# A float32 matmul with bias and tanh: another order of row tiles and column banks in the opening

## The chip, the cores and the metric

One core of one Trainium2 chip. The metric is the device time of one execution in microseconds (us); the profile's span is some 1.7 us shorter than it. "Product" below means one matmul instruction of 128x128 weights and 512 columns; the kernel needs 8192 of them (the last 32 are cut in two halves each).

## The reference

```python
def setup_inputs():
    m, k, n = 4096, 4096, 4096
    return {"a": randn(m, k), "b": randn(k, n), "bias": randn(n)}   # all float32; cut

def reference(a, b, bias):
    return np.tanh(np.matmul(a, b) + bias)
```

## The kernel before

A is loaded by GpSimd with a cast to fp16, transposed by VectorE in 32x32 blocks and held as `at` (k on the partitions). B's columns go in four groups of 1024, each two PSUM banks wide. Once a group of B is in SBUF, a row tile takes 64 products. The *opening* is the first 8 row tiles of the first column group: 512 products, made while B and A are still arriving, so it cuts k into pieces and keeps partial sums aside in SBUF (`spill`).

```python
    P, Q, QP, NB = 128, 4, 32, 512
    KT, MT, NCW, J = 32, 32, 1024, 2
    G = 4; KS = 8; AN = 3; BL = 4; KM = 16; WARM = 9
    ...
    def put_aside(ps, m, j):                      # first partial sum
        nc.scalar.copy(aside(m, j), ps)

    def add_aside(ps, m, j):                      # a further one
        nc.vector.tensor_tensor(out=aside(m, j), in0=ps, in1=aside(m, j), op=add)

    def end(ps, m, j):                            # last one: add, tanh, store
        finish(ps, aside(m, j), m, j * NB, o_sb=aside(m, j))

    def across(ps, ms, t0, nt, first):            # 4 rows x 2 banks, k tile by k tile
        for t in range(t0, t0 + nt):
            for m in ms:
                for j in range(J):
                    mm(ps[m][j], ats[m], b_cur, t, j, t == first, False)

    def group1(t0, t1, done, before):             # rows 4 to 7, one after the other
        for m in range(G, 2 * G):
            for j in range(J):
                ps = psum.tile([P, NB], fp32, name="ps")
                for t in range(t0, t1):
                    mm(ps, ats[m], b_cur, t, j, t == t0, t == t1 - 1)
                before(m, j)
                done(ps, m, j)

    for i in range(WARM):                         # products on zeros, to warm the array
        nc.tensor.matmul(warm, zeros[:, :P], zeros, start=i == 0, stop=i == WARM - 1)

    load_b_low(nc.sync, raw_b, 0, 0, 1)           # k tile 0 of B as float32
    nc.scalar.copy(b_cur[0][:, 0, :], raw_b[:, 0, :])
    for m in range(G):
        load_nat(m, 1)                            # A, k 0 to 4, by rows
    ...                                           # B k 1 to 2, A k 4 to 8, B k 3 to 6, ...
    turn_nat(0, 1, nc.vector.tensor_copy)         # transposed on TensorE
    turn_nat(1, 1, nc.scalar.copy)
    row(0, 0, 1)
    ...                                           # cut
    group1(KM, KT, end, before3)                  # last block: rows 4 to 7, k 16 to 32
```

`want(...)` puts a load in a list that GpSimd issues in order; a load of A waits for one of AN = 3 buffers. `turn(...)` is the VectorE transpose of a loaded piece.

## Time and profile before

| | before |
|---|---|
| median, 4 runs | 1785.2 us (1784.98 to 1785.65) |
| span of the profile | 1783.5 us |
| first product | 6.79 us |
| 65th product starts | 25.30 us |
| 513th product starts (opening over) | 121.99 us |
| from there to the last column | 1654.2 us, 0.2154 us each |

The prediction below shows the lines. The starts of the nth product are counted from the matmul records of the trace, of which none is missing; 512 products at 0.2158 us are 110.5 us. How to read them: TensorE is the chain from 23.73 us to the end, so only the opening's first 25 us can be shortened, and only if nothing later starts to wait. That condition is what this case is about.

### The profile page before, as it was taken

The page shows a single profiled execution, that of the slowest core. Times are in us where ns is not written, and L with a number is a line of the kernel's source. Part 1 is how long each engine was busy: PE and PEld are TensorE (multiplying, and loading weights), DVE is VectorE, ACT ScalarE, POOL GpSimd, SP SyncE. Part 2 cuts the span into 40 slices and gives each one's busy share as a digit, 9 for nine tenths or more (in the row PEclk, how much of TensorE's full clock was granted, in tenths as well). Part 3 has the DMA queues.
Part 4 walks back from the last instruction along what each step waited for, and adds up shares of the span by engine and source line. Part 5 has one row for each costly group of instructions (what it writes and reads, how often), then busy time and mean ns, then how long its engine had stood idle before and what let it go on. Part 6 is the DMA issues. An engine that isn't in the chain of part 4 may idle for free.

```text
span 1783.5 us, 20856 instructions
## 1 busy us (share of the span) xinstructions
PE 1774.8 (100%) x8257; PEld 807.3 (45%) x8257; DVE 768.3 (43%) x686; ACT 173.8 (10%) x279; POOL 865.1 (49%) x1611
## 2 busy tenths in 40 slices
PE   8999999999999999999999999999999999999999
PEld 3444444444444444444444444444444444444444
DVE  2864444344434443444434443444334443444342
ACT  2021000000000000000000000000000000000001
POOL 6455666544465445444455555444544454444510
PEclk9999999999999999999999999999999999999999
DMA  9999999876999967767699997766777667766731
GB/s 189 204 178 174 173 167 161 137 134 108 160 172 165 152 109 117 116 111 128 111 169 170 159 151 116 119 117 107 129 115 123 107 111 118 119 114 109 116 77 42
DMA packets 280321, 238.68 MB, mean 134 GB/s; under 512 B 157856, under 2 KB 230560, under 8 KB 280224
## 3 DMA queue, kind: packets, MB, share of 16 engines
q0 software_dynamic: 242784, 169.71, 69.5%
q1 hardware_dynamic: 37152, 67.52, 10.6%
q8 instruction: 64, 1.05, 0.2%
q14 instruction: 33, 0.27, 0.0%
q10 hardware_dynamic: 288, 0.13, 0.0%
HBM read 337.64 MB, written 67.11 MB: 227 GB/s over the span
## 4 chain that ended last, share of the span: by engine, by line
PE 98%; DMA 1%; issue 0%; POOL 0%; ACT 0%; DVE 0%; POOLq 0%; DVEq 0%
PE ps L415 93%; PE ps L138 6%; DMA b<-in_b_dram 1%; POOL nat L238 0%; ACT o_sb L152 0%; POOL b L69 0%; DVE o_sb L149 0%; PE tp L251 0%; POOL ident L257 0%; POOLq L257 0%; DVEq L149 0%; POOLq L438 0%
## 5 line engine op out<-in xcount | busy, mean ns | idle before, releaser
L415 PE MATMUL ps<-b,at 128*128 128x512 f16 x7712 | 1657.8, 378 | 0.0
L90 POOL DMA_DIRECT2D an<-in_a_dram x1488 | 800.2, 545 | 802.0 <-DVE at L100 570.0
L415 PEld LDWEIGHTS <-at 128*128 128x128 f16 x7712 | 754.6, 98 | 903.3
L100 DVE STREAM_TRANSPOSE at<-an 128x3072 f16<-128x3072 f16 (+2 forms) x376 | 563.1, 1548 | 50.5 <-DMA an<-in_a_dram 50.5
L149 DVE TENSOR_TENSOR o_sb<-ps,bias_bc 128x512 f32<-128x512 f32 (+1 forms) x243 | 165.8, 683 | 919.0 <-PE ps L415 711.4
L152 ACT ACTIVATE o_sb<-o_sb 128x512 f32<-128x512 f32 (+1 forms) x243 | 151.4, 624 | 1502.6 <-DVE o_sb L149 1496.6
L73 POOL DMA_DIRECT2D b<-in_b_dram x96 | 51.8, 544 | 17.8 <-DMA an<-in_a_dram 9.1
L138 PE MATMUL ps<-b,at 128*128 128x512 f16 x256 | 56.9, 379 | 3.0 <-DMA b<-in_b_dram 2.6
L138 PE MATMUL ps<-b,atx 128*128 128x512 f16 x256 | 55.7, 379 | 0.0
L138 PEld LDWEIGHTS <-at 128*128 128x128 f16 x256 | 24.7, 98 | 33.2 <-issue 3.5
L138 PEld LDWEIGHTS <-atx 128*128 128x128 f16 x256 | 25.1, 98 | 30.2
L100 DVE STREAM_TRANSPOSE atx<-an 128x512 f16<-128x512 f16 (+2 forms) x14 | 17.7, 1300 | 10.2 <-DMA an<-in_a_dram 10.2
L69 POOL DMA_DIRECT2D b<-in_b_dram x13 | 8.3, 641 | 22.3 <-PE ps L415 19.8
L152 ACT ACTIVATE spill<-spill 128x512 f32<-128x512 f32 x16 | 10.1, 630 | 76.8 <-DVE spill L149 76.8
L149 DVE TENSOR_TENSOR spill<-ps,spill 128x512 f32<-128x512 f32 x16 | 11.0, 687 | 15.1 <-PE ps L138 15.1
L175 DVE TENSOR_TENSOR spill<-ps,spill 128x512 f32<-128x512 f32 x16 | 10.2, 677 | 3.2 <-PE ps L138 3.2
L172 ACT COPY spill<-ps 128x512 f32<-128x512 f32 x16 | 8.8, 593 | 22.0 <-PE ps L138 21.9
L180 DVE TENSOR_TENSOR spill<-spill,bias_bc 128x512 f32<-128x512 f32 x16 | 9.7, 678 | 0.0
L225 PE MATMUL ps<-zeros 128*128 128x512 f16 x9 | 4.0, 631 | 1.3 <-DVE zeros L221 1.3
L252 DVE COPY atx<-tp 128x1024 f16<-128x1024 f16 x1 | 0.7, 692 | 7.2 <-PE tp L251 7.2
L252 DVE COPY at<-tp 128x512 f16<-128x512 f16 x2 | 0.8, 425 | 5.9 <-PE tp L251 5.9
L238 POOL DMA_DIRECT2D nat<-in_a_dram x5 | 2.8, 574 | 1.1 <-POOLq L438 0.8
(14 smaller groups left out, 12.4 us busy)
## 6 DMA issues: line engine op xcount, KB each, us to landing
an<-in_a_dram POOLq DMA_DIRECT2D x480, 192.0 KB, 4.9
out_dram<-o_sb SPq DMA_DIRECT2D x239, 256.0 KB, 2.4
an<-in_a_dram POOLq DMA_DIRECT2D x960, 32.0 KB, 2.6
b<-in_b_dram POOLq DMA_DIRECT2D x103, 256.0 KB, 8.3
b<-in_b_dram POOLq DMA_DIRECT2D x6, 1024.0 KB, 13.5
out_dram<-spill SPq DMA_DIRECT2D x16, 256.0 KB, 2.3
an<-in_a_dram POOLq DMA_DIRECT2D x28, 128.0 KB, 6.4
an<-in_a_dram POOLq DMA_DIRECT2D x12, 256.0 KB, 7.6
```

What stands on the lines that cost most here:

```text
L69: queue.dma_start(out=dst, in_=src[:, ds(t0 % BL, nt), :])
L73: nc.gpsimd.dma_start(out=bt[t0 // TB][ds(q * QP, QP), ds(t0 % TB, nt), :], in_=src.rearrange("(t p) n -> p t n", p=QP),)
L90: nc.gpsimd.dma_start(out=an[ds(q * QP, QP), :, ds((t - t0) * QP, n * QP)], in_=src.rearrange("(mb p) k -> p mb k", p=QP),)
L100: nc.vector.transpose(at[:, ds(t, n), :].rearrange("P t (mb p) -> P mb t p", p=QP), an[:, ds(mb0, Q), ds((t - t0) * QP, n * QP)].rearrange ...
L138: nc.tensor.matmul(ps, at[:, t, :], bt[t // TB][:, t % TB, ts(j, NB)], start=start, stop=stop)
L149: nc.vector.tensor_tensor(out=o_sb[:, piece], in0=ps[:, piece], in1=addend[:, piece], op=mybir.AluOpType.add)
L152: nc.scalar.activation(o_sb[:, piece], o_sb[:, piece], mybir.ActivationFunctionType.Tanh)
L172: nc.scalar.copy(aside(m, j), ps)
L175: nc.vector.tensor_tensor(out=aside(m, j), in0=ps, in1=aside(m, j), op=mybir.AluOpType.add)
L180: nc.vector.tensor_tensor(out=aside(m, j), in0=aside(m, j), in1=bias_bc[:, ts(j, NB)], op=mybir.AluOpType.add)
L225: nc.tensor.matmul(warm, zeros[:, :P], zeros, start=i == 0, stop=i == WARM - 1)
L415: nc.tensor.matmul(ps, at[:, t, :], b_cur[t // TB][:, t % TB, ds(c0, w)], start=t == 0, stop=t == KT - 1,)
```

## The change

Its intent: let TensorE begin with less data. Eight row tiles by one bank of columns use the same eight PSUM banks as four rows by two, but a step from bank 0 to bank 1 then needs only 0.5 MB of new data for 32 products. The first 0.5 MB of B (k 0 to 4 of bank 0) comes through SyncE as float32 and is cast by ScalarE, row tiles of A are worked on as they land. Sizes in MB are 2^20 bytes as written to SBUF, fp16 unless said otherwise.

```diff
-    G = 4
+    R = 8
+    H = R // 2
...
-    raw_b = spill[3]...[:, ds(0, 1), :]
-    load_b_low(nc.sync, raw_b, 0, 0, 1)
-    nc.scalar.copy(b_cur[0][:, 0, :], raw_b[:, 0, :])
+    raw = bpool.tile([P, BL, NB], fp32, name="raw", tag="b_3")
+    for t in range(0, BL, 2):
+        load_b_low(nc.sync, raw[:, ds(t, 2), :], 0, t, 2, NB)
+    for t in range(BL):
+        nc.scalar.copy(b_cur[0][:, t, :NB], raw[:, t, :])
...
+    want_a("a0", R - NN, NN * P, (R - NN) * Q, 0, BL)      # rows 6 and 7
+    want(lambda: load_b_bank_low(1, 0, 2))
+    want(lambda: load_b_bank_low(1, 2, 2))
+    want(lambda: load_b_bank_low(1, BL, BL))
+    want_half(0, BL, BL)                                   # A of rows 0 to 3
+    want_half(1, BL, BL)                                   # A of rows 4 to 7
+    want(lambda: load_b_bank_low(0, BL, BL))
+    want_half(0, 8, 4)
+    want(lambda: load_b_bank(0, 8, 4))
+    want_half(1, 8, 4)
+    want_half(0, 12, 4)
+    want(lambda: load_b_bank(0, 12, 4))
+    want_half(1, 12, 4)
+    want(lambda: load_b_bank(1, 8, 4))
+    want(lambda: load_b_bank(1, 12, 4))
+    want(lambda: load_bias(bias_bc, 0, nc.gpsimd))
+    for t in (KM, KM + 8):
+        want(lambda t=t: load_b_bank(1, t, 4))
+        want_half(0, t, 8)
+        want(lambda t=t: load_b_bank(1, t + 4, 4))
+        want_half(1, t, 8)
+    for t in range(KM, KT, 4):
+        want(lambda t=t: load_b_bank(0, t, 4))
...
+    for m in rows:                                         # bank 1, k 24 to 32
+        row(ps, m, 1, KM + 8, KT, done=end)
...
-    group1(KM, KT, end, before3)
+    for i, m in enumerate([*range(H, R), *range(H)]):      # last block: bank 0, k 16 to 32
+        row(ps, m, 0, KM, KT, start=True, done=end)
+        if i in (2, 5):
+            new_at(i // 3)
```

The visits are, as (bank, k): (0, 0 to 4), (1, 0 to 8), (0, 4 to 16), (1, 8 to 32), (0, 16 to 32).

## The prediction

> **What bounds the kernel now.** I read the page first, then the chain that ended last in order of time, then the timeline of TensorE over the first 30 us, then two windows. From the page:
>
> ```profile
> span 1783.5 us, 20856 instructions
> PE 1774.8 (100%) x8257; PEld 807.3 (45%) x8257; DVE 768.3 (43%) x686; ACT 173.8 (10%) x279; POOL 865.1 (49%) x1611
> PE 98%; DMA 1%; issue 0%; POOL 0%; ACT 0%; DVE 0%; POOLq 0%; DVEq 0%
> ```
>
> TensorE is 98% of the chain. Nothing outside TensorE can be worth more than the other 2%. The chain in order of time says where those are:
>
> ```profile
> 4.47 6.72 DMA b<-in_b_dram
> ...
> 12.86 8.71 DMA b<-in_b_dram
> 21.57 0.04 issue
> 21.61 1.67 PE ps L138 x7
> 23.29 0.45 PE tp L251 x8
> 23.73 98.42 PE ps L138 x456
> 122.15 1654.20 PE ps L415 x7680
> ```
>
> From 23.73 us on TensorE runs without a wait: 456 matmuls in 98.42 us and 7680 in 1654.20 us, 0.2158 and 0.2154 us each. Before 23.73 us the chain goes through loads of B. The timeline of TensorE there (start, length, engine, line, count, idle time before with its releaser):
>
> ```profile
> 5.08 0.63 PE L251 MATMUL tp<-ident,nat 128*128 128x128 f16 x4
> 6.54 0.41 PE L251 MATMUL tp<-ident,nat 128*128 128x128 f16 x4 [0.83 <-DMA nat<-in_a_dram]
> 6.79 0.59 PE L138 MATMUL ps<-b,at 128*128 128x512 f16 x2
> ...
> 9.14 4.35 PE L138 MATMUL ps<-b,at 128*128 128x512 f16 x18 [0.25 <-ACT at L252]
> 15.31 5.56 PE L138 MATMUL ps<-b,at 128*128 128x512 f16 x25 [1.83 <-DMA b<-in_b_dram]
> 21.61 1.67 PE L138 MATMUL ps<-b,at 128*128 128x512 f16 x7 [0.74 <-DMA b<-in_b_dram]
> 23.12 0.61 PE L251 MATMUL tp<-ident,nat 128*128 128x128 f16 x8
> 23.57 1.89 PE L138 MATMUL ps<-b,at 128*128 128x512 f16 x8
> 25.30 4.91 PE L138 MATMUL ps<-b,atx 128*128 128x512 f16 x22
> ```
>
> The first real matmul starts at 6.79 us and 64 are done at 25.30 us. At 0.2158 us, 64 take 13.8 us, so 4.7 us of these 18.5 us are lost: 2.57 us in the two named waits for B, the rest in 16 transposes (0.4 to 0.6 us a group) and matmuls whose operand was just copied. So the budget has three parts: 6.79 us before the first product, 4.7 us lost to 25.30 us, and some 3.7 us after the last matmul (1783.5 minus 1779.83, where TensorE's last piece ends). The third is untouched. The ideal gain of any opening is a few us of 1785: 2% would be 35.7 us.
>
> The rate of the loads sets the opening:
>
> ```profile
> 6.79:23.73 16.94, 13.97 (x76) 6.33 (x75) 2.91 (x5) 2.88 (x6) 10.13 (x18) 1.00 1.35 188
> 23.73:122.15 98.42, 98.42 (x458) 44.64 (x456) 67.17 (x79) 16.54 (x28) 51.01 (x94) 1.00 1.14 197
> ```
>
> The last figures are the DMA share and GB/s as written (fp16, so twice that is read): the engines are full throughout, and TensorE still keeps up after 25 us, if each byte comes in the right order. Summing the trace's packets of the GpSimd queue by their ends: 0.25 MB by 5.4 us, 0.5 by 7.0, 0.75 by 8.6, 1.0 by 10.1, 1.5 by 13.1, 2.0 by 15.6, 2.5 by 18.1, 3.0 by 20.6, 3.5 by 23.5, 14.25 by 78.3. An instruction sees its data 0.4 to 1 us after the last packet.
>
> **What the Trainium skill says.** (1) "TensorE: Matmul & The Clock Gate", Back-to-back issue gap: the isolated gap of warm matmuls of 512 columns is about 216 ns. The trace agrees (0.2154 to 0.2158 us), so the change's 8192 matmuls cost the same. The same section gives 131 ns for sustained streams; this trace shows nothing near it. (2) "DMA: Bandwidth & Descriptors", SWDGE vs HWDGE vs iDMA: a cast inside a DMA is only possible from GpSimd. That is why B through SyncE arrives as float32 and needs ScalarE copies. (3) The same page, Issuing engines are not separate DMA queues: queues share the same 16 engines. The trace agrees: in the us where both queues were busy (3.5 to 4.5 us) SyncE's wrote 148 KB and GpSimd's 124 KB, against some 340 and 170 KB alone.
>
> **The change part by part.**
>
> *Removed.* The order of 4 rows by 2 banks. For its first 32 products it needed 512 rows of B by 1024 columns, 1 MB as fp16, and 0.5 MB of A; for 64, 3 MB; these are what the two waits are for.
>
> *Added.* Eight rows by one bank: the first 32 products need 1 MB of A and 0.5 MB of B, the second 32 only 0.5 MB more of B, the third 1 MB of A and 0.5 MB of B, the fourth 0.5 MB of B. So 64 products need 2.0 MB instead of 3, and 128 need 4 in both. B's first 0.5 MB is 1 MB of float32 by SyncE, 0.5 MB more than before in that form.
>
> *Loads.* SyncE's first half should be there at 4.4 us as its 0.5 MB was before; the second half costs 0.5/0.34 = 1.5 us of engine time, shared with GpSimd's loads, so it comes at some 7 us and the GpSimd curve above shifts by up to 1.5 us. With 0.9 us to landing: A's first rows at 5.4, 7.2, 8.2, 9.3, 10.1 and 10.9 us; rows 6 and 7 (0.25 MB) 12.4; B's second bank, first halves, 13.9 and 15.4, then 18; A of k 4 to 8 for rows 0 to 3 20.5, rows 4 to 7 23.0; B bank 0 of these 25.9 us.
>
> *ScalarE.* Four casts of 128x512 instead of one of 128x1024 that took 1.05 us: about 0.55 each, done by about 5.5 and 8.7 us. Evictions take 0.59 us alone (8 in a row took 4.23), under a row's 0.86 us. *VectorE:* six copies of 0.42 us, two small transposes of about 0.65 us. Both lie beside TensorE.
>
> *TensorE.* Row 1's transposes start at 7.2 us. Row 0 k 0 to 1 from 7.5, row 1 from 8.1 (its copy), row 2's transposes to 9.0, k 2 to 3 of rows 0 and 1 to 9.9; then rows 2, 3, 4 at 0.86 + 0.3 to 0.4 us for the next row's transposes, to 13.5; rows 5, 6, 7 at 0.86, to 16.1 us. Each row's data are there by then. Bank 1 for all rows: 32 times 0.216 = 6.9 us, to 23.0 us, its last B having come at 15.4. The third block has its A at 20.5 and 23.0 plus 0.65 to 2.6 us of VectorE, needed at 23.0 and 26.5.
>
> Sum: 64 products at 23.0 us instead of 25.3, gain 2.3 us, and no transpose of TensorE after it in either kernel. The 8128 products left and the end are the same. 1785.3 minus 2.3 = 1783.0 us.
>
> **The rivals.**
>
> *A. A wait later in the opening.* A of k 8 to 16 now comes in runs of 4 k tiles (256 B written; packets of that size went at 177 KB/us, 512 B at 194, 2 KB at 208) and B in 1 KB (195 KB/us). I put some 57 us between 3.5 and 14.25 MB, slightly slower than before's 54.8. Estimated margins: k 16 to 24, rows 4 to 7: loaded 65, needed 71; k 24 to 32, rows 4 to 7: 82 with its transpose, needed 85; bank 0 of k 16 to 32: 90, needed piece by piece from 91.7. In that last stretch eight outputs of 256 KB go out (before, 8 of them went in 90 to 97 us), which may cost B 3 us. For: the margin there is about zero. Against: the kernel before had no wait at all after 25 us at nearly the same load. This would give back 1 to 4 us: 1784 to 1787.
>
> *B. SyncE's float32 starves A.* If SyncE's queue takes the larger share, row 1 lands after 7.5 us and everything slips by 1 us; if GpSimd's does, k 2 to 3 comes at 9 to 10 us. Either takes 0.5 to 1.5 us: 1783.5 to 1784.5.
>
> *C. PSUM or the buffers.* Eight rows use all eight banks, and a stage's row m waits for the eviction of its row m of the stage before. A stage goes row by row, so seven rows lie between (6 us against 0.7). Against it also: VectorE's in-order transposes precede the evictions, but their loads are due before. Spill tiles take slots of tiles read for the last time in the first block. I expect no wait. If one of these were wrong at every stage change: +5 us.
>
> *D. A better start.* If rows come as early as before (6.5 us), the gain is 3.5 to 4: 1781.5.
>
> **Range and chances.** Centre 1783.0. D gives 1781, A and C at their likely sizes up to 1786.5; 8 in 10: 1780.8 to 1786.2. Faster by 2% is impossible by the budget (15 us in all): 0.005. Slower by 2% needs 36 us of new waits in a 120 us opening whose loads are the same: 0.015. Within 2%: 0.98.
>
> **What would show it.** In the changed profile: first product at about 7.5 us; casts of 128x512 near 4.5 and 7 us; the 65th product at 23.0 plus or minus 1 us; no wait of TensorE for B over 0.5 us before it; from there one unbroken piece in the chain of waits to the last column. The prediction is wrong if TensorE waits for A or B between 23 and 120 us (rival A), if the first block ends after 17 us (B), if TensorE waits for VectorE or ScalarE at a stage change (C), or if the time per matmul is not 0.2154 to 0.2158 us.

## The result, and the profile after

| | before | after |
|---|---|---|
| median, 4 runs each | 1785.2 us | 1786.67 us |
| lowest to highest | 1784.98 to 1785.65 | 1784.24 to 1788.93 |
| ratio, after over before | | 1.0008 (95%: 0.999 to 1.0025) |

A ratio is the mean time of one kernel's runs over that of the other's runs of the same rounds, so not quite the ratio of the medians quoted. The median lies 0.5 us above the predicted range, and the spread of the kernel after is 4.7 us where that of before is 0.7. The profile is of its slowest run (1788.93 us). Its page:

```profile
span 1787.2 us, 20871 instructions
PE 1777.3 (99%) x8257; PEld 807.9 (45%) x8257; DVE 764.8 (43%) x693; ACT 174.2 (10%) x280; POOL 883.2 (49%) x1629
PE 94%; DMA 4%; POOL 1%; issue 1%; ACT 0%; DVE 0%; DVEq 0%; POOLq 0%
```

TensorE is 94% of the chain where it was 98%: the chain now runs through loads for much longer. The chain in order of time shows how long (start, length, what):

```profile
46.93 7.59 DMA bias_bc<-in_bias_dram
...
77.95 7.67 DMA an<-in_a_dram
85.62 1.56 issue
87.18 4.28 POOL b L74 x8
91.47 7.40 DMA b<-in_b_dram
98.87 0.14 issue
99.00 26.88 PE ps L139 x116
125.89 1654.20 PE ps L391 x7680
```

Before, TensorE's unbroken piece began at 23.73 us; now it begins at 99.00 us, released by a load of B. From there the rest is the same to a hundredth: 1654.20 us. So the whole difference lies in the opening. TensorE's timeline of the kernel after:

```profile
7.08 0.62 PE L236 MATMUL tp<-ident,nats 128*128 128x128 f16 x4 [1.80 <-DMA nats<-in_a_dram]
8.08 0.61 PE L236 MATMUL tp<-ident,nats 128*128 128x128 f16 x4 [0.38 <-DMA nats<-in_a_dram]
8.49 1.91 PE L139 MATMUL ps<-b,atx 128*128 128x512 f16 x4
...
17.23 1.89 PE L139 MATMUL ps<-b,atx 128*128 128x512 f16 x8
...
24.19 3.63 PE L139 MATMUL ps<-b,atx 128*128 128x512 f16 x16
...
80.46 7.08 PE L139 MATMUL ps<-b,atx 128*128 128x512 f16 x32 [0.84 <-DVE atx L101]
87.38 9.66 PE L139 MATMUL ps<-b,at 128*128 128x512 f16 x44
99.00 13.07 PE L139 MATMUL ps<-b,at 128*128 128x512 f16 x52 [1.97 <-DMA b<-in_b_dram]
```

The two waits for B before 25 us are gone, and the 65th product starts at 24.19 us instead of 25.30. But two new waits stand at 80.46 us (A of k 24 to 32 for rows 0 to 3, turned late by VectorE) and 99.00 us (the last piece of B's first bank). Why the first of them was late, VectorE's timeline shows:

```profile
69.84 4.62 DVE L101 STREAM_TRANSPOSE at<-an 128x1024 f16<-128x1024 f16 x4 [3.33 <-DMA an<-in_a_dram]
74.39 4.86 DVE L183 TENSOR_TENSOR spill<-spill,bias_bc 128x512 f32<-128x512 f32 x8
79.17 4.62 DVE L101 STREAM_TRANSPOSE atx<-an 128x1024 f16<-128x1024 f16 x4
```

The last load of that A was in at 77.67 us (the chain above: 70.00 + 7.67), but VectorE had the bias additions of bank 1 ahead of it in its program and turned it only from 79.17 us. Those additions themselves stood behind A of rows 4 to 7, which landed just before 69.84 us. So this wait comes from late loads and from the place of the additions together; 1.5 us of it is the additions.

And 52 products from 99.00 us end at 111.91, where the next piece starts: 12.9 us for what takes 11.2 at 0.2158. The windows around it say why; the last three figures are the granted clock, the DMA share and GB/s:

```profile
90.00:95.00 5.00, 5.00 (x25) 2.29 (x24) 5.00 (x9) 4.02 (x7) 3.58 (x7) 1.00 1.09 140
95.00:100.00 5.00, 3.04 (x13) 1.14 (x12) 4.99 (x9) 0.82 (x2) 2.80 (x6) 0.91 1.17 289
100.00:105.00 5.00, 5.00 (x18) 1.96 (x17) 0.69 (x1) 0.63 (x1) 3.10 (x6) 0.74 1.24 289
```

The granted clock is 0.91 and 0.74 there. The trace's clock record has it at one half from 99.15 us for 3.41 us: the wait of 2 us was answered by a halved clock just as the data arrived. The Trainium skill, "TensorE: Matmul & The Clock Gate", Part 1, describes such a gate, half rate after an idle window of some 3.4 us; the length of the period, 3.41 us, agrees, but here 2 us of idle time were enough (see e5).

The ledger of this profile, each term as the distance between products less 0.2158 us: start of the 65th product 1.1 us earlier; wait at 80 us 1.0 us; wait at 99 us 2.1 us; half clock 1.7 us. Sum +3.7 us, and the spans differ by 1787.2 - 1783.5 = 3.7 us.

**When the loads are in.** Summing the packets of GpSimd's queue by their ends gives, for the same number of MB:

| MB | 0.125 | 0.5 | 1.5 | 2.5 | 3.5 | 7 | 11 | 14.25 | 16 |
|---|---|---|---|---|---|---|---|---|---|
| before, us | 4.6 | 7.0 | 13.1 | 18.1 | 23.5 | 41.8 | 61.6 | 78.3 | 88.2 |
| after, us | 6.2 | 8.5 | 14.3 | 20.8 | 27.3 | 48.2 | 68.2 | 85.4 | 97.6 |

The queue after is 1.5 us late from the start, 4 us at 3.5 MB and 7 us at 14.25 MB. The table is not yet a cause: before, the last 2 MB hold only A for rows 4 to 7, due later.

### The profile page after: what moved, and what is told of

Its sections match the earlier page's. It is cut to its first block, busy times and chain, and to the rows that moved or that the text cites. A ratio compares the mean times of both kernels' runs of the same rounds, so it can differ in the third digit from the quotient of the medians.

```text
span 1787.2 us, 20871 instructions
## 1 busy us (share of the span) xinstructions
PE 1777.3 (99%) x8257; PEld 807.9 (45%) x8257; DVE 764.8 (43%) x693; ACT 174.2 (10%) x280; POOL 883.2 (49%) x1629
## 4 chain that ended last, share of the span: by engine, by line
PE 94%; DMA 4%; POOL 1%; issue 1%; ACT 0%; DVE 0%; DVEq 0%; POOLq 0%
PE ps L391 93%; DMA an<-in_a_dram 2%; PE ps L139 2%; DMA b<-in_b_dram 1%; POOL b L74 1%; POOL an L91 0%; DMA bias_bc<-in_bias_dram 0%; DMA nats<-in_a_dram 0%; POOL b L70 0%; ACT o_sb L153 0%; POOL nats L231 0%; DVE o_sb L150 0%; DVEq L150 0%; POOLq L414 0%
## 5 line engine op out<-in xcount | busy, mean ns | idle before, releaser
L101 DVE STREAM_TRANSPOSE at<-an 128x3072 f16<-128x3072 f16 (+2 forms) x382 | 564.4, 1528 | 16.2 <-DMA an<-in_a_dram 16.2
L74 POOL DMA_DIRECT2D b<-in_b_dram x120 | 65.3, 550 | 11.5 <-issue 5.3
L101 DVE STREAM_TRANSPOSE atx<-an 128x512 f16<-128x512 f16 (+1 forms) x20 | 16.7, 892 | 19.9 <-DMA an<-in_a_dram 19.9
L70 POOL DMA_DIRECT2D b<-in_b_dram x10 | 7.4, 743 | 20.5 <-PE ps L391 19.6
L150 DVE TENSOR_TENSOR spill<-ps,spill 128x512 f32<-128x512 f32 x16 | 10.3, 677 | 11.4 <-PE ps L139 11.4
L178 DVE TENSOR_TENSOR spill<-ps,spill 128x512 f32<-128x512 f32 x8 | 4.8, 673 | 0.0
```

The lines of the kernel that those rows point to most:

```text
L70: queue.dma_start(out=dst, in_=src[:, ds(t0 % BL, nt), :])
L74: nc.gpsimd.dma_start(out=bt[t0 // TB][ds(q * QP, QP), ds(t0 % TB, nt), ds(c0, w)], in_=src.rearrange("(t p) n -> p t n", p=QP),)
L101: nc.vector.transpose(at[:, ds(t, n), :].rearrange("P t (mb p) -> P mb t p", p=QP), an[:, ds(mb0, Q), ds((t - t0) * QP, n * QP)].rearrange ...
L150: nc.vector.tensor_tensor(out=o_sb[:, piece], in0=ps[:, piece], in1=addend[:, piece], op=mybir.AluOpType.add)
```

## The experiments

**The theories.** *L*: the new opening's loads are slower, for their small pieces, and TensorE runs into them. *Q*: a form of it, that GpSimd holds back small loads while a large one is under way. *S*, the rival: only the start counts and the rest is noise. Two more were formed: *H*, that part of the first block runs at half clock, and *D*, that the load order's deadlines matter more than its rate.

All edits are to the kernel after unless said otherwise. All sixteen gave correct results, each with five runs beside nine runs of the kernel before on the same chip. The columns: median and spread; the median of before; then of the profiled run the starts of the 33rd, 65th and 513th product. The runs were made in four calls on three chips (e1 to e4; e5 to e8; e9 to e12; e13 to e16), so medians are best compared within a call, or with the kernel before of the same call.

| run | median (lowest to highest) | before | 33rd | 65th | 513th |
|---|---|---|---|---|---|
| e1_again | 1786.44 (1785.9 to 1789.45) | 1785.39 | 17.46 | 24.37 | 126.25 |
| e2_a8 | 1784.88 (1784.67 to 1786.57) | 1785.39 | 18.84 | 25.75 | 122.44 |
| e3_split | 1786.58 (1784.91 to 1789.01) | 1785.39 | 17.27 | 24.18 | 121.73 |
| e4_sync_half | 1783.98 (1782.23 to 1787.41) | 1785.39 | 17.93 | 24.83 | 124.14 |
| e5_warm | 1787.7 (1785.49 to 1788.63) | 1785.3 | 15.95 | 23.85 | 125.45 |
| e6_before_narrow | 1785.5 (1784.96 to 1785.97) | 1785.3 | 16.69 | 24.95 | 121.64 |
| e7_a8_warm | 1784.89 (1784.51 to 1787.72) | 1785.3 | 16.24 | 23.77 | 122.85 |
| e8_a8_sync | 1786.69 (1784.92 to 1789.73) | 1785.3 | 17.21 | 24.12 | 122.91 |
| e9_chunk | 1784.88 (1783.92 to 1785.53) | 1785.52 | 17.64 | 24.55 | 122.35 |
| e10_chunk_warm | 1783.26 (1782.9 to 1784.66) | 1785.52 | 15.84 | 22.74 | 120.08 |
| e11_chunk_a8_bias | 1784.12 (1783.48 to 1785.54) | 1785.52 | 16.83 | 23.74 | 120.43 |
| e12_all | 1783.95 (1783.44 to 1787.98) | 1785.52 | 15.36 | 22.27 | 120.19 |
| e16_again_2 | 1785.44 (1784.64 to 1789.26) | 1785.62 | 17.57 | 24.48 | 122.78 |
| e15_chunk_warm_2 | 1783.85 (1783.69 to 1785.17) | 1785.62 | 15.89 | 22.80 | 120.52 |
| e13_late_loads_warm | 1783.96 (1783.05 to 1787.0) | 1785.62 | 15.56 | 22.47 | 120.13 |
| e14_all_warm | 1783.53 (1782.97 to 1785.23) | 1785.62 | 16.76 | 24.01 | 121.96 |

No interval of a ratio excludes 1: the smallest ratios are 0.9989, of e10 (0.9976 to 1.0001) and e14 (0.9975 to 1.0002). So the argument rests on the profiles' waits and on sets of runs that do not overlap, not on the ratios.

### e1_again: no edit

> The changed kernel again, unedited, as the yardstick of this call. Theory L (loads): the new opening finishes its first 64 products about 1 us earlier than before, but its loads run later than before from 15 us on (14.25 MB of the GpSimd queue by 85.4 us against 78.3), so TensorE waits near 80 and 96 us, and a wait of about 2 us there is followed by 3.4 us at half clock. It expects 1784 to 1789 us, with the spread of the four runs known. Theory S (start): only the first block matters, and the four runs known are noise: 1784 to 1785 with a spread under 1 us.

Measured: 1786.44 us with a spread of 3.6 us, nine runs of before beside it within 1.2. In its profile TensorE waited 3.4 us for the last B at 99.5 us and was at half clock twice, from 8.1 and 100.3 us. The pattern of the first profile repeats, and the spread belongs to the kernel. S in its simple form (1784 to 1785, spread under 1) is out.

### e2_a8: A of k 8 to 16 in larger pieces

```diff
-    want_half(0, 8, 4)
+    want_half(0, 8, 8)
     want(lambda: load_b_bank(0, 8, 4))
-    want_half(1, 8, 4)
-    want_half(0, 12, 4)
+    want_half(1, 8, 8)
     want(lambda: load_b_bank(0, 12, 4))
-    want_half(1, 12, 4)
```

(and the transposes to match)

> A of k 8 to 16 in pieces of 8 k tiles (packets of 512 B) instead of 4 (256 B), nothing else. Theory L with packet size as the cause: 2 MB at about 194 instead of 175 KB per us, so all later loads come some 1.1 us earlier, the waits near 80 and 96 us shrink by that much, 1 to 3 us faster than the unedited kernel (about 1784). Theory Q (issue order: at most eight GpSimd loads under way, so small loads behind a large one leave the queue short): fewer and larger pieces help as well, up to 2 us. Theory S: no difference.

Measured: 1784.88 us, 1.6 under e1. 7 MB are in at 45.0 us, against 46.8 (e1) and 48.2 (after); 14.25 MB at 83.1 against 84.2 and 85.4. TensorE has no wait after the first block. The chain that ended last, in order of time:

```profile
15.55 107.05 PE ps L139 x496
122.60 1654.20 PE ps L387 x7680
```

One unbroken piece from the first block to the end, though the first block itself was slow (the 33rd product at 18.84 us; see e5). Larger pieces do bring the data sooner, by 1.1 to 1.9 us against e1 (16 MB at 93.8 us against 97.2), and in this profile the waits are gone. TensorE also came 1.4 us later to them (65th product at 25.75 us), which helps. L and Q both predict it.

### e3_split: the two 512 KB loads of B halved

```diff
-    want(lambda: load_b_bank_low(1, BL, BL))
+    want(lambda: load_b_bank_low(1, BL, 2))
+    want(lambda: load_b_bank_low(1, BL + 2, 2))
...
-    want(lambda: load_b_bank_low(0, BL, BL))
+    want(lambda: load_b_bank_low(0, BL, 2))
+    want(lambda: load_b_bank_low(0, BL + 2, 2))
```

> The two loads of 512 KB of B for k 4 to 8 are each cut into two of 256 KB; packets, bytes and order stay. Theory Q: GpSimd's wait of 4.4 us at 20.7 us shrinks to under 2, 3.5 MB of the queue are in by 26 us instead of 27.3, and the kernel gets 1 to 2 us faster. Theory L with packet size as the cause: the wait of GpSimd changes, but the rate stays at some 160 to 175 KB per us between 15 and 28 us, and the time stays within 0.5 us of the unedited kernel.

GpSimd's waits up to 60 us, in the kernel after and then in e3 (total us, times, longest):

```profile
POOL an L91 <- DMA b<-in_b_dram: 5.1, 2, 4.4
```

```profile
POOL an L91 <- DMA b<-in_b_dram: 2.3, 3, 1.3
```

The wait that Q named shrinks from 4.4 to 1.3 us, and 3.5 MB are in at 25.2 us against 26.3 (e1) and 27.3 (after). So GpSimd does hold back loads behind a large one, worth about 1 us of loading here. The time did not follow: 1786.58 us. Q is real and small.

### e4_sync_half: half of B's first bank by SyncE, half by GpSimd

```diff
-    for t in range(0, BL, 2):
-        load_b_low(nc.sync, raw[:, ds(t, 2), :], 0, t, 2, NB)
-    for t in range(BL):
+    load_b_low(nc.sync, raw[:, ds(0, 2), :], 0, 0, 2, NB)
+    for t in range(2):
...
         load_nat(m)
+        if m == 1:
+            load_b_bank_low(0, 2, 2)
```

> SyncE brings only k 0 to 1 of B's first bank as float32; k 2 to 3 come as fp16 through GpSimd after the second row tile of A. If the second float32 load is what made the first row tile land at 7.1 us instead of 5.0, the first transposes start by 5.5 us and the first product by 7.2 (8.5 in the changed kernel), 64 products are done by about 23.2 us instead of 24.2, and all loads are 0.5 to 1.5 us earlier, which shortens the later waits too: 1 to 3 us faster. If it is not (A lands late because its six loads share one tile or for its own order), the start stays at 7 us.

TensorE's timeline of e4:

```profile
5.44 0.61 PE L235 MATMUL tp<-ident,nats 128*128 128x128 f16 x4 [0.16 <-DMA nats<-in_a_dram]
6.92 0.41 PE L235 MATMUL tp<-ident,nats 128*128 128x128 f16 x4 [0.86 <-DMA nats<-in_a_dram]
...
9.29 0.55 PE L235 MATMUL tp<-ident,nats 128*128 128x128 f16 x4 [0.83 <-DMA nats<-in_a_dram]
9.63 1.91 PE L139 MATMUL ps<-b,atx 128*128 128x512 f16 x4
```

The first transposes start at 5.44 us instead of 7.08, the first product at 7.17 instead of 8.49: SyncE's second load did delay A. GpSimd's first packet starts at 3.54 us here as in the kernel before (3.50), and at 4.49 in the kernel after, though GpSimd issued the load at 1.3 us in all three. But the 65th product starts at 24.83 us, not 23.2: row tile 2 now comes behind more of B (the wait at 9.29), and the clock was halved from 9.42 us for 3.41 us, which the four products in 1.91 us show. The median is 1783.98 us and the spread 5.2, the widest of all runs.

### e5_warm: 14 warm-up matmuls instead of 9

```diff
-    WARM = 9
+    WARM = 14
```

> The changed kernel with 14 warm-up matmuls on zeros instead of 9, nothing else; they end by about 6 to 7.4 us, when A's first row tile lands. Theory H (half clock): in the five profiles taken of the changed kernel and its variants the array ran part of the first block at half clock (until 10 to 14 us, or from about 8 to 12 us), because it idled from 5.3 us to the first product at 7.2 to 8.5 us; the kernel before was at full clock from 6.0 us on. Filling that idle time should keep or raise the clock: the 65th product starts at about 23 us instead of 24.2 to 25.7, and the time falls by 0.5 to 1.5 us against the unedited changed kernel (1786.4). Without H: no change, or 0.3 us slower where the warm-up outlasts the landing.

TensorE alone from 8.20 to 11.50 us, in e1 and then in e5 (busy, count, granted clock, DMA share, GB/s):

```profile
8.20:11.50 3.30, 3.30 (x12) 0.50 1.45 178
```

```profile
8.20:11.50 3.30, 3.30 (x25) 1.00 1.46 181
```

At the same loading rate twice as many instructions pass. H's step is right in its effect: in the five profiles with 14 warm-ups and the whole float32 bank by SyncE (e5, e7, e10, e13, e15) the 33rd product starts at 15.6 to 16.2 us, in the seven with 9 (after, e1, e2, e3, e9, e11, e16) at 16.8 to 18.8; none of the five has a half-clock period after its first full-clock one until the end of the program. Each of the seven ran part of the first block at half clock, but in two ways. In three the array was not yet at full clock: the clock record has it there only from 10.3 to 13.8 us (10.40 in the profile after). In the other four it was, from 4.7 to 5.4 us, and lost it again for 3.41 us.

The clock records say more than H does. In all 18 profiles the clock changes only at whole multiples of 3.413 us from one another (88.75 us are 26 of them, 1778.34 us are 521). Adding up TensorE's idle time (as the timelines count it) within each such period at full clock, from the start to 130 us, the eight that were followed by half clock held 1.7 to 2.6 us of it, and none with 1.63 us or less was; between 1.7 and 1.9 us both happened (1.83 us in the kernel before: no). So the place of a wait counts, not only its length: the 2.0 us before 99.00 us in the profile after lie in one period, the 2.6 us before 100.41 us in e5 in two, 1.63 and 1.00 us, and e5 kept its clock. Where the periods begin differs from profile to profile, which no kernel here chose: that part is luck.

But H's time is wrong: 1787.7 us, no gain. TensorE's timeline shows where it went:

```profile
23.85 3.63 PE L139 MATMUL ps<-b,atx 128*128 128x512 f16 x16 [0.83 <-DVE atx L101]
53.28 6.20 PE L139 MATMUL ps<-b,atx 128*128 128x512 f16 x28 [0.77 <-DMA b<-in_b_dram]
81.20 7.08 PE L139 MATMUL ps<-b,atx 128*128 128x512 f16 x32 [1.00 <-DVE atx L101]
```

and 2.8 us more before 100.41 us for the last B. What TensorE gains in the first block it hands back, because what comes later does not come earlier: the opening is set by its loads. (They were also the latest of all profiles here, 7 MB at 49.3 us, so this one profile can't tell the two apart; e9 and e10 can.)

### e6_before_narrow: the small loads put into the kernel before

```diff
         for q in (0, 2, 1, 3):
-            load_b(b_cur, 0, t0, nt, q)
+        for j in range(J):
+            for q in (0, 2, 1, 3):
+                load_b(b_cur, 0, t0, nt, q, j * NB, NB)
```

(to the kernel before; `load_b` takes a column offset and width as in the kernel after)

> The kernel before with one thing of the change put in: B of k 8 to 32 of the first column is loaded one bank at a time, in packets of 1 KB and loads of 128 KB instead of 2 KB and 256 KB, same bytes, same order of computing. Theory L (small loads are slower): 14.25 MB of the GpSimd queue are in at 80 to 83 us instead of 78.3, and TensorE gets a wait of 0.5 to 2 us between 80 and 95 us that the kernel before does not have; 1785.5 to 1788. If the order of rows and banks alone makes the later waits (and not the load pieces), the kernel stays at 1785.4 without a wait after 25 us.

Measured: the loads are later as L expects (14.25 MB at 80.5 us against 78.3, 16 MB at 90.5 against 88.2), and the time does not change at all: 1785.5 beside 1785.3 us. The chain in order of time:

```profile
23.38 98.42 PE ps L138 x456
121.80 1654.20 PE ps L416 x7680
```

No wait after 23.38 us. Loads that are 2 us later cost the order of before nothing. They are fewer than the 7 us of the kernel after, but even at its pace (14.75 MB in at 88.1 us) the bytes due at the start of the last block of before, at 94 us, would be in time. So slower loads alone do not explain the waits of the kernel after; what counts is how much each order needs by when. That led to theory D: before, the last block (from 94 us) works row by row on A of rows 4 to 7, for which B is long in (14.25 MB) and each row adds 0.5 MB in 6.9 us. After, the first row of the last block, 3.5 us long, already needs the last k tile of B's bank: all of 16 MB.

### e7_a8_warm: e2 and e5 together

```diff
-    WARM = 9
+    WARM = 14
-    want_half(0, 8, 4)
+    want_half(0, 8, 8)        # and so on, as in e2
```

> The changed kernel with A of k 8 to 16 in pieces of 8 k tiles and 14 warm-up matmuls. If both effects are real and separate, they add: no wait near 80 and 99 us and the 65th product at 23 us, 1783 to 1784 us, spread under 2 us.

Measured: 1784.89 us, the same as e2. The first block was quick (16.24 us), but TensorE then waited 0.6 us at 23.8 us and 1.6 us at 42.6 us, the first for a load of A, the second for a transpose of VectorE. The expected sum of the two effects missed: what the start gained went into the next waits, as in e5.

### e8_a8_sync: e2 and e4 together

```diff
+    load_b_low(nc.sync, raw[:, ds(0, 2), :], 0, 0, 2, NB)    # as in e4
+    want_half(0, 8, 8)                                       # as in e2
```

> The changed kernel with A of k 8 to 16 in pieces of 8 k tiles and only k 0 to 1 of B's first bank through SyncE. The loads are then early from the start (0.25 MB of A by 5.6 us) and the later waits gone: 1782 to 1783.5 us; the slower runs should be those with a half-clock period in the first block.

Measured: 1786.69 us: a miss of 3 us. In its profile the clock was halved from 8.17 us in the first block, and TensorE waited 1.3 us at 42.7 us. The profile is of a run of 1786.18 us; what made the run of 1789.73 us slow was not seen.

### e9_chunk: the last block in chunks of k

```diff
+    for t in range(KM, KT - 4, 4):
+        for m in range(H, R):
+            row(ps, m, 0, t, t + 4, start=t == KM)
     for i, m in enumerate([*range(H, R), *range(H)]):
-        row(ps, m, 0, KM, KT, start=True, done=end)
+        if m >= H:
+            row(ps, m, 0, KT - 4, KT, done=end)
+        else:
+            row(ps, m, 0, KM, KT, start=True, done=end)
```

> The changed kernel with the last block of the opening (bank 0, k 16 to 32) in another order only: rows 4 to 7 go together through four chunks of 4 k tiles, in four PSUM banks, instead of row by row; rows 0 to 3 as they were. The loads stay as they are. Theory D (deadline): in the changed kernel the first row of that block needs the last of B's first bank (16 MB of the GpSimd queue, in at 97 to 98 us) about 3.5 us after the block starts at some 95 us, while the kernel before needs only about 14.75 MB by then and gets the rest of A while it computes. With chunks the last piece is due some 10 us after the block's start. So the wait at about 97 to 99 us and the half-clock period after it go: 2 to 4 us faster than the unedited changed kernel (1786.4), 1783 to 1785, spread under 2 us; the wait near 80 us may stay. If the later waits are a plain lack of loading rate, the wait moves to the next piece of data and the time does not change.

TensorE's timeline of e9:

```profile
80.90 7.08 PE L139 MATMUL ps<-b,atx 128*128 128x512 f16 x32 [0.94 <-DVE atx L101]
87.81 20.88 PE L139 MATMUL ps<-b,at 128*128 128x512 f16 x96
108.53 13.98 PE L139 MATMUL ps<-b,atx 128*128 128x512 f16 x64
```

The wait near 99 us and the half clock after it are gone, with the loads no faster than in the profile after (16 MB at 98.2 us, 97.6 there); the wait near 80 us, which the edit does not touch, stays. 1784.88 us, spread 1.6: inside the range expected, but 1.6 us under e1 and not 2 to 4. This is the run that tells L from D: nothing about a load was changed, only when its data are due. The opening is 24.55 + 448 x 0.2158 + 1.1 = 122.3 us, measured 122.35.

### e10_chunk_warm: the chunks and 14 warm-ups

```diff
-    WARM = 9
+    WARM = 14                 # with the edit of e9
```

> The same with 14 warm-up matmuls, which brought the first block to 15.9 us but was eaten by later waits. With the last wait gone, theory H expects up to 0.5 to 1 us less than with the chunks alone; if the wait for A of k 24 to 32 near 80 us still sets the pace, there is no difference, since that wait takes back what the start gains.

Measured: 1783.26 us; its five runs (1782.9 to 1784.66) all lie under the nine of before (1784.85 to 1786.16). The wait near 80 us is 0.4 us in this profile. The warm-up, worth nothing alone, is worth 1.6 us here: more than expected, and it is the start of the 65th product, 22.74 instead of 24.55 us.

### e11_chunk_a8_bias and e12_all: later loads, and SyncE's half

```diff
-    want(lambda: load_bias(bias_bc, 0, nc.gpsimd))
     for t in (KM, KM + 8):
         want(lambda t=t: load_b_bank(1, t, 4))
         want_half(0, t, 8)
+        if t > KM:
+            want(lambda: load_bias(bias_bc, 0, nc.gpsimd))
```

(with e9; A of k 8 to 16 as in e2, its stage now one piece of k 8 to 16 per row, B ahead of A's second half; `add_bias` of bank 1 moved behind the transpose of that A. e12 adds the edit of e4.)

> Chunks, A of k 8 to 16 in pieces of 8 k tiles with their stage done in one piece per row, and the bias (0.5 MB, 2 us of the queue) loaded behind A of k 24 to 32 for rows 0 to 3 instead of before all of k 16 to 32. Everything that TensorE waited for near 80 us comes 2 to 4 us earlier, so there is no wait after the first block: 1782.5 to 1784, spread under 1.5 us.

> All of that and only k 0 to 1 of B's first bank by SyncE. If the start sets the time once the later waits are gone, another 0.5 to 1.5 us: 1781.5 to 1783.

Measured: 1784.12 us and 1783.95 us. e11 has no wait after the first block, as expected; whether that is due to the earlier loads or to the bias additions no longer standing before the transpose is not separated, since the edit does both. Its time is no better than e10's, since its first block was slow (16.83, at 9 warm-ups). e12 has the earliest 65th product of all, 22.27 us, with 9 warm-ups and no half clock after 4.79 us (TensorE idled 1.2 us in the period after that), then two waits of 0.6 us near 37 and 44 us; its median misses the range expected by 1 us, and one of its five runs took 1787.98 us at a granted clock of 0.998.

### e16_again_2, e15_chunk_warm_2, e13_late_loads_warm, e14_all_warm: side by side

e16 is the kernel after, e15 is e10 again. The edits of the other two, against the kernel after:

```diff
-    WARM = 9
+    WARM = 14                 # e13: e11 with this
+    WARM = 12                 # e14: e12 with this
```

> The changed kernel unedited, on the same chip and against the same runs of the kernel before as the three that follow: 1786 to 1787.5 us with a spread of 2 to 4 us.

> Chunks in the last block and 14 warm-up matmuls, again. If deadline and half clock together are the missing gain: 1783 to 1784 us, some 3 us under the unedited changed kernel and 2 under the kernel before, spread under 2 us. If the earlier result was luck of the chip: within 1 us of the unedited one.

> The same with A of k 8 to 16 in pieces of 8 k tiles and the bias later. If the wait of 0.2 to 1.0 us near 80 us is all that is left after the first block: 0.2 to 1 us faster than without (1782.5 to 1783.2). If nothing is left there, the same.

> Everything, with SyncE bringing only k 0 to 1 and 12 warm-up matmuls. If SyncE's second load still costs the start 0.5 to 1 us: 1781.8 to 1782.8. If the start is then set by the third row tile and by k 2 to 3, which come later in this order: no better than without, 1783.

Measured on one chip: 1785.44 (spread 4.6), 1783.85 (1.5), 1783.96 (4.0) and 1783.53 us (2.3), beside 1785.62 for before. The medians of e16 and e15 differ by 1.6 us, not the 3 expected, because e16 came out lower than expected; e15 is 1.8 us under before. The chain of e15:

```profile
77.82 1.17 DVE atx L101
78.98 0.05 issue
79.03 41.65 PE ps L139 x192
120.68 1654.20 PE ps L397 x7680
```

Its opening is 22.80 + 96.7 + 1.0 (the wait near 79 us) = 120.5 us, measured 120.52. e13 takes that wait away and has another of 0.7 us at 44 us: no gain. e14 starts its transposes at 5.30 us, but its second row tile was 2 us behind (7.69 us), so its first product came at 7.94 us, no earlier than without. With the same loads e12 had it at 6.69 us; so the start of this order varies by over 1 us from run to run, and one profile of each does not say what 12 warm-ups are worth in it.

## Why the prediction was right or wrong

Right in part: the two waits for B are gone, the 65th product starts earlier (by 1.1 us, not 2.3), the time per product at full clock did not change, the budget of a few us held. Wrong in the step after it: "the 8128 products left and the end are the same", with "one unbroken piece in the chain" after the 65th product. In their place the profile after has two waits, 1.0 and 2.1 us, and 1.7 us of half clock: 4.8 us where the prediction had none. Three of the signs that it named for being wrong came: waits for A or B between 23 and 120 us (rival A), the first block ending after 17 us (B, 17.23), and TensorE waiting for VectorE (C). Rival A was named with its size, 1784 to 1787 us, and given too little weight. The median is 0.5 us above the range; how far is partly luck, since the same kernel's median in e16 was 1785.44 us, inside it. Point by point:

- **The start.** Predicted: A's first tile at 5.4 us, first product at 7.5. Measured 7.08 and 8.49 (7.6 to 8.4 for the product in the other profiles with SyncE's whole bank). The step "shared with GpSimd's loads" failed: SyncE's first 0.5 MB were in at 4.0 us as before, but GpSimd's first packet came at 4.49 us instead of 3.50, when SyncE's queue had already written 0.7 MB of its 1 MB (0.8 to 0.9 in the other profiles). e4 shows that the second load is the cause; why the queues did not take turns from the start is not shown. It is rival B, of the size given there. (For the us from 3.5 to 4.5 in the kernel before, counting each packet over its time gives 130 and 125 KB, not the prediction's 148 and 124.)
- **The first block and the 65th product.** Predicted 16.1 and 23.0 us; measured 17.2 and 24.2 in the profile after, and 15.9 and 22.7 to 22.8 in e10 and e15. The sum had **no term for the array's clock**. The prediction took 0.216 us for every product of the first block; in every profile with 9 warm-ups and SyncE's whole bank the clock was at half for part of it (until 10.40 us in the profile after), because the warm-up ended at 5.3 us and TensorE idled for most of the time to some 8 us. A half-clock period of 3.41 us costs up to 1.7 us; with the clock repaired the predicted 23.0 us is met in spite of the later start.
- **The later loads: the step that failed.** Rival A put bank 0 of k 16 to 32 at 90 us, or 93 with the outputs, and needed from 91.7 us. Measured: 97.6 us in the profile after, 16 MB of the queue. Of the mis-sized 7.6 us, 2.3 were there at 3.5 MB (27.3 instead of 25.0), 1.1 came in the stretch to 14.25 MB (58.1 us instead of 57: that term was right), and some 4 in the last 1.75 MB, which took 12.1 us (3 of these 4 are what the prediction allowed for the outputs).
- **The argument against rival A.** "The kernel before had no wait at all after 25 us at nearly the same load" compared totals. e6 and e9 show that it should have compared deadlines: before needs 14.75 MB when its last block starts at 94 us, and has them at 81; after needs all 16 MB 3.5 us into its last block, which also starts at 94 us. The margin was some 13 us in one order and below zero in the other, at the same bytes. The prediction listed due times for the kernel after only.
- **The half clock after a wait.** Absent from all the rivals. A wait of 2.1 us cost 3.8 in the profile after. It goes with the spread of the runs: in the three profiles of the unedited kernel (after, e1, e16) the wait for the last B was 2.1, 3.4 and 1.6 us, the first two were answered by half clock, and the spans are 1787.2, 1787.7 and 1784.2 us. For the runs that were not profiled this is not shown.
- **Rival C** (PSUM, evictions, VectorE's order) was rightly given little for PSUM: no profile shows TensorE waiting for ScalarE or for an eviction at a stage change. But its other half came: "VectorE's in-order transposes" did hold TensorE, at 80.46 us, since the prediction left out the eight bias additions (4.86 us) that stand before the transposes of A of k 24 to 32.

What stays open: why the last 1.75 MB took 12.1 us. GpSimd's loads were late there too (the chain goes through a load of A of 7.67 us, 1.56 us of issue and eight issues of B), which may be Q again, but no experiment took that stretch alone. The outputs are not all of it: in the profile after GpSimd's queue wrote some 195 KB (of 1024 bytes) per us up to 88 us, 98 to 177 from there to 95 us, and only then did the first output move. With A of k 8 to 16 in larger pieces (e2, e7, e8, e11 to e14) the stretch took 9.6 to 10.7 us, without 10.3 to 13.0. The wait near 80 us was not tested by moving the bias additions alone. The slow single runs of e8, e12 and e13 were not profiled.

## What to carry to other kernels

When an order of work is changed in a stage that runs against its loads, write down for both orders how many bytes are due at each block's start, not how many are loaded in all: an earlier start is worth nothing if a later block's first row needs the last byte. Chunking that block so that the last byte is due late kept the gain that a faster start alone only moved into the next wait. Ask the same of an engine that works in order: what stands before the work that is due. And cover the time to the first data with warm-up work up to its landing, since a product at half clock costs twice (0.427 us instead of 0.2158).

The best version run, the change with the last block in chunks and 14 warm-ups (e10 and e15), gave 1783.26 and 1783.85 us, 2.3 and 1.8 us under the kernel before. All five runs of e10 and four of five of e15 lie under all nine of before; at 0.1% the intervals of the ratios do not exclude 1.

## What the Trainium skill lacked or had wrong

- "TensorE: Matmul & The Clock Gate", Why this matters for your kernels: it asks for no idle gap over some 3 us between bursts. In the profile after a gap of 2.1 us ended in a half-clock period of 3.41 us that cost 1.7 us more, and in e1 one of 3.4 us did too, while 2.8 us in e5 and 2.0 us in the kernel before did not. A gap of 2 us can be enough, not always: what went before a half clock was 1.7 to 2.6 us of idle time within one period of 3.413 us (see e5).
- The same page, Part 1: it calls the ramp under 1% of a typical kernel and advises against fitting a count of cold matmuls. Under 1% holds here, yet it is as large as what the change could win, 2.3 us by the prediction: the 33rd product at 15.6 to 16.2 us with 14 warm-ups, 16.8 to 18.8 with 9.
- The same page, Back-to-back issue gap: 131 ns sustained for 512 columns; here 215.4 ns over 7680 matmuls, close to the 216 the section calls isolated.
- "DMA: Bandwidth & Descriptors", Issuing engines are not separate DMA queues: the queues interleave, but not from the first packet. With 1 MB on SyncE's queue GpSimd's first packet started at 4.5 to 5.2 us, with 0.5 MB at 3.5 to 3.7, after the same issue at 1.3 us.
- No page has the rates of casting loads by size of the written packet: in the kernel before 177 KB per us at 256 B, 194 at 512 B, 195 at 1 KB, 208 at 2 KB.
